# The first load of a batched product, made in eight transfers of 16 rows

## The chip, the core and the metric

The kernel runs on one core of a Trainium2 chip. Its metric is the device time of one execution in microseconds, the median of the runs shown. The core has five engines that run their own instruction queues: TensorE (PE), VectorE (DVE), ScalarE (ACT), GpSimd (POOL) and SyncE (SP). Data moves between the chip's main memory (HBM) and the on-chip memory of 128 partitions (SBUF) by 16 DMA engines; a transfer is issued from the queue of SyncE or ScalarE, and counts a semaphore up when it has landed.

## The reference

x and y have the shape 8 x 12 x 512 x 64, the result 8 x 12 x 512 x 512, all in float32:

```python
def reference(x, y):
    return np.einsum('bhtc,bhsc->bhts', x, y).astype(np.float32)
```

So there are 96 products of a 512 x 64 matrix with a 64 x 512 matrix. Inputs are 25.17 MB, the output is 100.66 MB.

## The kernel before, in words

The 96 products are taken in 6 groups of 16. Of each group there is one load of x and one of y, 12 loads in all, each 128 partitions x 4096 floats (2 MB, 16 KB for each partition, contiguous in HBM). Load n is of x for even n and of y for odd n. The results leave in 48 stores of the same size, 64 x 2 rows of 16 KB.

Loads and results share five buffers of 128 x 4096 floats (`slots`), handed out in turn by `slot()`. Each slot has a semaphore of its own for its transfers, `dma0` to `dma4`; a transfer adds 16 to it. The helper `emit` keeps books on who wrote and read what: before an instruction it puts the waits that it needs, and after it the semaphore increment. `ticks` holds the count that each semaphore will have reached, and a consumer waits for that count.

The order of the work is written out. `load(0)` to `load(4)` come first on SyncE's queue and need no wait, since the slots are empty. Then, for n from 0 to 11, `compress(n)` turns a load into bfloat16: ScalarE copies a load of x from its slot into `xk` (line 113), and a load of y is copied into `yb` in four pieces, two on VectorE, one on GpSimd, one on ScalarE. `mix` copies pieces of `xk` into `xb` so that pairs of values interleave; in the first part this is on GpSimd. When `compress(n)` has emptied a slot, `load(n + 5)` is issued into it: load 5 goes into slot 0 after ScalarE's copy of load 0.

`transposes` turns `xb` and `yb` on VectorE into the operands of the products, and `result` makes the products for one store: two times four matrix products of 128 x 512 (line 202) into PSUM, two copies from PSUM into a slot, mostly on ScalarE (line 113), and a store of the slot, from SyncE for two results in three and from ScalarE's queue for the third (and the last four).

The steps that the change touches are `load` (lines 127 to 134), of it the case n = 0, and through the semaphore count the wait of the instructions that read slot 0 (`copy`, line 110, and `need`, line 71).

Of the kernel before, what the change touches and what calls it, by code (L numbers as in the profile page):

```python
# [9 lines left out]
def kernel(  # L10
# [22 lines left out]
    nc = tc.nc  # L33
# [9 lines left out]
    K = 8  # L43
    E = R // K
    D = 32
    SLOTS = 5
    fp32 = mybir.dt.float32
    bf16 = mybir.dt.bfloat16
    u32 = mybir.dt.uint32
    COPY = mybir.ActivationFunctionType.Copy  # L50
    assert C == 2 * D and S == T and R == 2 * D and Q * V == D

    xv = x.rearrange("b h t c -> (b h t c)").rearrange("(g p n) -> g p n", p=P, n=R * C)
    yv = y.rearrange("b h t c -> (b h t c)").rearrange("(g p n) -> g p n", p=P, n=R * C)
# [5 lines left out]
    ps = ctx.enter_context(tc.tile_pool(name="ps", bufs=1, space=bass.MemoryType.PSUM))  # L60
    slots = [sb.tile([P, K * S], fp32, name=f"slot{i}") for i in range(SLOTS)]
    xks = [sb.tile([P, R, C], bf16, name=f"xk{i}") for i in range(NG - 1)]
    ybs = [[sb.tile([P, R // 2 * D], u32, name=f"yb{h}{i}") for i in range(NG - 1 + h)] for h in range(2)]
    xbs = [sb.tile([P, K * E * D], u32, name=f"xb{half}") for half in range(2)]
    xTs = [sb.tile([P, K * D * E], u32, name=f"xT{i}") for i in range(2)]
    yTs = [sb.tile([P, D * R // 2], u32, name=f"yT{i}") for i in range(2)]
    pms = [ps.tile([P, 4, S], fp32, name=f"pm{i}") for i in range(2)]
    engines = {"act": nc.scalar, "dve": nc.vector, "pool": nc.gpsimd, "pe": nc.tensor, "sp": nc.sync}
    sems, ticks, known, snaps, writer, readers = {}, {}, {e: {} for e in engines}, {}, {}, {}

    def need(name, points):

        best = {}
        for p, v in points:
            if known[name].get(p, 0) < v:
                best[p] = max(best.get(p, 0), v)
        for p, v in list(best.items()):
            if any(snaps[q, w].get(p, 0) >= v for q, w in best.items() if q != p):
                del best[p]
        for p, v in best.items():  # L80
            engines[name].wait_ge(sems[p], v)  # L81
            known[name][p] = v
            for q, w in snaps[p, v].items():
                known[name][q] = max(known[name].get(q, 0), w)

    def emit(name, make, reads=(), writes=(), dma=None):

        points = [writer[r] for r in (*reads, *writes) if r in writer]
        points += [v for w in writes for v in readers.get(w, ())]
        if name == "pool" and name in ticks:  # L90
            points.append((name, ticks[name]))
        need(name, points)
        p, step = (name, 1) if dma is None else (f"dma{dma}", 16)
        if p not in sems:
            sems[p] = tc.alloc_semaphore(p)
        make().then_inc(sems[p], step)
        at = (p, ticks.get(p, 0) + step)
        ticks[p] = at[1]
        snaps[at] = {**known[name], p: at[1]}
        if dma is None:  # L100
            snaps[at][name] = at[1]
        for r in reads:
            readers.setdefault(r, []).append(at)
        for w in writes:
            writer[w], readers[w] = at, []
# [14 lines left out]
    def both(i):  # L120
        return [("slot", i, 0), ("slot", i, 1)]

    def slot():
        made_slots.append(len(made_slots) % SLOTS)
        return made_slots[-1]

    def load(n):
        i = loaded[n] = slot()
        emit(
            "sp",  # L130
            lambda: nc.sync.dma_start(slots[i], (yv if n % 2 else xv)[n // 2]),  # L131
            writes=both(i),
            dma=i,
        )

    def compress(n):

# [8 lines left out]
        for half in range(2):  # L146
            b = g % (NG - 1 + half)
            yv2 = ybs[half][b].bitcast(bf16).rearrange("p (j c w) -> p j w c", j=R // 2, w=2)
            for ch in range(2):
                copy(  # L150
                    in_front[2 * half + ch],
                    yv2[ch * 64:(ch + 1) * 64],
                    ys[half * 64:(half + 1) * 64, :, ch * D:(ch + 1) * D].rearrange(
                        "p (j w) c -> p j w c", w=2
# [90 lines left out]
    with tc.tile_critical():  # L245
        for g in range(SLOTS):
            load(g)
        for half, name in enumerate(("dve", "pool")):
# [3 lines left out]
                writes=[("xb", half, part) for part in range(4)],  # L252
            )
        front = []
        for n in range(2 * NG):
            if n == 11:
                result(3, slot())
            compress(n)
            mix(n // 4, "pool", n % 4)
            if n == 4:  # L260
                transposes(0)
            if n < 5:
                load(n + SLOTS)
            elif n in (6, 8):
                load(n // 2 + 7)
            elif n < 10:
                front.append(slot())
            if n > 7 and n < 11:
                result(n - 8, front[n - 8])
            if n == 9:  # L270
                transposes(1)
# [38 lines left out]
```

## Time and profile before

| what | value |
|---|---|
| device time, median of 3 runs | 300.76 us (300.71 to 301.03) |
| span of the profiled execution, first to last instruction | 299.3 us |
| ScalarE / VectorE / TensorE / GpSimd busy | 204.2 / 160.8 / 131.2 / 56.0 us |
| DMA | 125.90 MB, mean 421 GB/s over the span |
| HBM read / written | 25.17 MB / 100.66 MB |
| first issue of a load | 0.95 us after the span's start |
| first copy of a landed load (ScalarE, xk) | 8.81 us |

The page gives busy times of each engine, then the span in 40 equal slices with the busy share in tenths, then the DMA queues. Of the profiled execution only the span is recorded; the time of a run is longer by what lies around the span, 300.76 - 299.3 = 1.46 us against the median. The timeline gives instructions in order of time, and the windows give the busy times and the moved bytes of chosen stretches. "SPq" marks an issue on SyncE's queue; "x <- y" is read "x written from y".

### The profile page before, as it was taken

The page shows a single profiled execution, that of the slowest core. Times are in us where ns is not written, and L with a number is a line of the kernel's source. Part 1 is how long each engine was busy: PE and PEld are TensorE (multiplying, and loading weights), DVE is VectorE, ACT ScalarE, POOL GpSimd, SP SyncE. Part 2 cuts the span into 40 slices and gives each one's busy share as a digit, 9 for nine tenths or more (in the row PEclk, how much of TensorE's full clock was granted, in tenths as well). Part 3 has the DMA queues.
Part 4 walks back from the last instruction along what each step waited for, and adds up shares of the span by engine and source line. Part 5 has one row for each costly group of instructions (what it writes and reads, how often), then busy time and mean ns, then how long its engine had stood idle before and what let it go on. Part 6 is the DMA issues. An engine that isn't in the chain of part 4 may idle for free.

```text
span 299.3 us, 1170 instructions
## 1 busy us (share of the span) xinstructions
PE 131.2 (44%) x384; PEld 35.2 (12%) x384; DVE 160.8 (54%) x77; ACT 204.2 (68%) x105; POOL 56.0 (19%) x23
## 2 busy tenths in 40 slices
PE   0000040557756665454655545464646473755100
PEld 0000010111111111111111111111111111111000
DVE  2167897999839590940946729219276330501400
ACT  1665676999999885677776868595959595459000
POOL 2399999991000000000000000000000000000000
PEclk9999999999599978596859597959597959587755
DMA  7999999999999999999999999999999999999995
GB/s 272 429 427 434 431 425 427 429 431 427 434 434 429 429 431 428 431 434 431 427 434 428 429 434 429 429 427 436 425 425 429 427 434 423 425 423 429 431 431 239
DMA packets 8645, 125.90 MB, mean 421 GB/s; under 512 B 960, under 2 KB 960, under 8 KB 960
## 3 DMA queue, kind: packets, MB, share of 16 engines
q1 hardware_dynamic: 6048, 88.08, 69.3%
q10 hardware_dynamic: 2592, 37.75, 29.6%
q8 instruction: 3, 0.05, 0.1%
q14 instruction: 2, 0.02, 0.0%
HBM read 25.17 MB, written 100.66 MB: 420 GB/s over the span
## 4 chain that ended last, share of the span: by engine, by line
DMA 57%; ACT 22%; PE 7%; issue 4%; DVE 3%; SPq 0%; ACTq 0%
DMA out_dram<-slot 44%; ACT slot L113 19%; DMA slot<-in_y_dram 7%; PE pm L202 7%; DMA slot<-in_x_dram 6%; DVE yb L115 2%; DVE slot L115 1%; ACT xk L113 1%; ACT yb L113 1%; SPq L131 0%; ACTq L81 0%; SPq L305 0%; SPq L245 0%
## 5 line engine op out<-in xcount | busy, mean ns | idle before, releaser
L113 ACT ACTIVATE slot<-pm 128x2048 f32<-128x2048 f32 x92 | 166.6, 1883 | 50.1 <-DMA out_dram<-slot 40.8
L202 PE MATMUL pm<-yT,xT 128*128 128x512 bf16 x384 | 131.2, 485 | 146.6 <-ACT slot L113 108.6
L180 DVE STREAM_TRANSPOSE xT<-xb 128x2048 uint32<-128x2048 uint32 x12 | 46.7, 3890 | 71.0 <-PE pm L202 68.6
L202 PEld LDWEIGHTS pm<-yT,xT 128*128 128x128 bf16 x384 | 35.2, 112 | 242.1 <-ACT slot L113 141.4
L115 DVE COPY xb<-xk 32x2048 bf16<-32x2048 bf16 x36 | 46.9, 1304 | 1.0
L115 DVE CAST yb<-slot 64x2048 bf16<-64x2048 f32 x12 | 36.1, 3012 | 17.0 <-DMA slot<-in_y_dram 16.8
L115 POOL COPY xb<-xk 32x2048 bf16<-32x2048 bf16 x12 | 36.2, 3019 | 10.5 <-ACT xk L113 9.7
L113 ACT ACTIVATE xk<-slot 128x4096 bf16<-128x4096 f32 x6 | 21.7, 3617 | 16.4 <-DMA slot<-in_x_dram 16.4
L115 DVE COPY slot<-pm 128x2048 f32<-128x2048 f32 x4 | 9.0, 2286 | 29.3 <-PE pm L202 29.3
L189 DVE STREAM_TRANSPOSE yT<-yb 128x1024 uint32<-128x1024 uint32 x12 | 23.2, 1932 | 0.0
L113 ACT ACTIVATE yb<-slot 64x2048 bf16<-64x2048 f32 x6 | 14.8, 2461 | 5.1 <-DMA slot<-in_y_dram 5.1
L115 POOL CAST yb<-slot 64x2048 bf16<-64x2048 f32 x6 | 17.8, 2968 | 1.3 <-DMA slot<-in_y_dram 0.8
L251 DVE MEMSET xb<- 128x2048 uint32 x1 | 1.8, 1765 | 1.4 <-SPq L245 1.4
L251 POOL MEMSET xb<- 128x2048 uint32 x1 | 1.8, 1804 | 0.5 <-SPq L245 0.5
L113 ACT ACT_TABLE_LOAD x1 | 1.3, 1283 | 0.9 <-SPq L245 0.9
L294 POOL MEMSET const-float32-0.0<- 128x1 f32 x1 | 0.1, 98 | 0.2 <-issue 0.2
L294 POOL MEMSET const-float32-1.0<- 128x1 f32 x1 | 0.1, 98 | 0.0
L294 POOL MEMSET const-bfloat16-1.0<- 128x1 bf16 x1 | 0.1, 98 | 0.0
L294 POOL MEMSET const-uint8-127<- 128x1 uint8 x1 | 0.1, 97 | 0.0
## 6 DMA issues: line engine op xcount, KB each, us to landing
out_dram<-slot SPq DMA_DIRECT2D x30, 2048.0 KB, 17.0
out_dram<-slot ACTq DMA_DIRECT2D x18, 2048.0 KB, 14.8
slot<-in_x_dram SPq DMA_DIRECT2D x6, 2048.0 KB, 17.6
slot<-in_y_dram SPq DMA_DIRECT2D x6, 2048.0 KB, 20.8
```

The source lines that it names most:

```text
L113: lambda: nc.scalar.activation(dst, src, COPY)
L115: else engines[name].tensor_copy(dst, src),
L180: lambda: nc.vector.transpose(xTs[half].rearrange("p (k r e) -> p k e r", k=K, e=E), xbs[half].rearrange("p (k e c) -> p k e c", k=K, e=E),),
L189: lambda: nc.vector.transpose(yTs[half].rearrange("p (r j) -> p j r", r=D), ybs[half][b].rearrange("p (j c) -> p j c", c=D),),
L202: last = nc.tensor.matmul(pms[k // 4][:, j, :], xT[:, k + j, h, :], yT[:, h * S:(h + 1) * S], start=True, stop=True,)
L251: lambda: engines[name].memset(xbs[half], 0.0),
L294: nc = _bacc.Bacc("TRN2", target_bir_lowering=False, num_devices=1)
```

## The change

Load 0, the first one of x, is issued as eight transfers instead of one. Transfer r (0 to 7) takes the partitions r, r + 8, r + 16, ..., r + 120: 16 rows of 16 KB. All eight add 16 to the semaphore of slot 0; the first seven do it directly, and `ticks` is set so that `emit` counts 128 for the last one. Every reader of slot 0 that waited for 16 waits for 128, and later counts of this semaphore are larger by 112. The other loads are as before.

```diff
+    W = 8
...
     def load(n):
         i = loaded[n] = slot()
-        emit(
-            "sp",
-            lambda: nc.sync.dma_start(slots[i], (yv if n % 2 else xv)[n // 2]),
-            writes=both(i),
-            dma=i,
-        )
+        src = (yv if n % 2 else xv)[n // 2]
+
+        def parts():
+
+            if n:
+                return nc.sync.dma_start(slots[i], src)
+            for r in range(W - 1):
+                nc.sync.dma_start(slots[i][r::W], src[r::W]).then_inc(sems["dma0"], 16)
+            ticks["dma0"] = 16 * (W - 1)
+            return nc.sync.dma_start(slots[i][W - 1::W], src[W - 1::W])
+
+        emit("sp", parts, writes=both(i), dma=i)
```

The order of the instructions on each engine's queue is otherwise the same: on SyncE the eight issues (lines 137 and 139 of the changed kernel) stand where the one stood (line 131), ahead of the four other first loads (line 135).

## The prediction

> **What bounds the kernel now.** I read the page's line of DMA shares and rates first, because the five engines are all far from full (ScalarE, the busiest, 68%).
>
> ```profile
> span 299.3 us, 1170 instructions
> ...
> PE 131.2 (44%) x384; PEld 35.2 (12%) x384; DVE 160.8 (54%) x77; ACT 204.2 (68%) x105; POOL 56.0 (19%) x23
> ...
> DMA  7999999999999999999999999999999999999995
> GB/s 272 429 427 434 431 425 427 429 431 427 434 434 429 429 431 428 431 434 431 427 434 428 429 434 429 429 427 436 425 425 429 427 434 423 425 423 429 431 431 239
> DMA packets 8645, 125.90 MB, mean 421 GB/s; under 512 B 960, under 2 KB 960, under 8 KB 960
> ```
>
> Of 40 slices only the first and the last are below nine tenths; the 38 between move 423 to 436 GB/s. The transfers never pause, so the time is: when the data begins to flow at full rate, plus 125.9 MB at that rate, plus the tail. Anything that costs transfer time in the first load is paid in full at the end, since no later slice has idle DMA time to take it up; and a compute engine that starts later costs nothing until it lets the queue of transfers run dry.
>
> Next the opening, by the windows of the first microseconds. After window and length come PE, PEld, DVE, ACT and POOL, the clock, the DMA share (above 1 because a packet is booked where it starts) and GB/s.
>
> ```profile
> 1.00:2.00 1.00, 0.00 (x0) 0.00 (x0) 0.56 (x1) 1.00 (x1) 1.00 (x1) 1.00 0.09 33
> 2.00:3.00 1.00, 0.00 (x0) 0.00 (x0) 1.00 (x1) 0.18 (x1) 0.75 (x1) 1.00 1.57 279
> 3.00:4.00 1.00, 0.00 (x0) 0.00 (x0) 0.21 (x1) 0.00 (x0) 0.00 (x0) 1.00 0.49 197
> 4.00:5.00 1.00, 0.00 (x0) 0.00 (x0) 0.00 (x0) 0.00 (x0) 0.00 (x0) 1.00 1.00 426
> ...
> 7.00:8.00 1.00, 0.00 (x0) 0.00 (x0) 0.00 (x0) 0.00 (x0) 0.00 (x0) 1.00 1.04 442
> 8.00:9.00 1.00, 0.00 (x0) 0.00 (x0) 0.00 (x0) 0.19 (x1) 0.00 (x0) 1.00 0.92 393
> 9.00:10.00 1.00, 0.00 (x0) 0.00 (x0) 0.00 (x0) 1.00 (x1) 0.00 (x0) 1.00 1.11 475
> ```
>
> Data flows from about 2.0 us, but until 4.0 us at (279 + 197) / 2 = 238 GB/s, a little over half. This is the only stretch in which the DMA engines have work and do not deliver.
>
> Last, the timelines of SyncE's queue and of ScalarE (start, duration, what).
>
> ```profile
> 0.95 0.39 SPq L131 DMA_DIRECT2D slot<-in_x_dram  x1
> 1.40 0.42 SPq L131 DMA_DIRECT2D slot<-in_y_dram  x1
> 1.86 0.43 SPq L131 DMA_DIRECT2D slot<-in_x_dram  x1
> 2.33 0.66 SPq L131 DMA_DIRECT2D slot<-in_y_dram  x1
> 3.04 0.49 SPq L131 DMA_DIRECT2D slot<-in_x_dram  x1
> 12.46 0.33 SPq L131 DMA_DIRECT2D slot<-in_y_dram  x1
> ```
>
> ```profile
> 8.81 3.62 ACT L113 ACTIVATE xk<-slot 128x4096 bf16<-128x4096 f32 x1 [6.63 <-DMA slot<-in_x_dram]
> 13.69 2.44 ACT L113 ACTIVATE yb<-slot 64x2048 bf16<-64x2048 f32 x1 [1.26 <-DMA slot<-in_y_dram]
> 18.58 3.62 ACT L113 ACTIVATE xk<-slot 128x4096 bf16<-128x4096 f32 x1 [2.45 <-DMA slot<-in_x_dram]
> ```
>
> The five first loads are issued by 3.53 us and land one after another: ScalarE starts on them at 8.81, 13.69, 18.58, so one load of 2,097 KB takes 4.89 us, 429 GB/s. Load 5 is issued at 12.46, when ScalarE has emptied slot 0.
>
> **The change, part by part.** The sum is made against this execution: its span is 299.3, the median of the three timed runs is 300.76, so 1.46 us lie around the span; I keep them and add every difference to 300.76.
>
> *The rate of the first load.* Before, load 0 has 33 + 279 + 197 = 509 KB moved by 4.00 us, and the other 1,588 KB take 1,588 / 429 = 3.70 us: done at 7.70. Afterwards the same 128 rows of 16 KB move, but as sets of 16 whose partitions are 8 apart. Every transfer in this trace covers all 128 partitions, so no row shows whether 16 rows at that spacing are taken in at 429 GB/s. The bounds are the fastest and the slowest rates that the trace has under load. Fast end: 429 from the first byte, 2,064 / 429 = 4.81 us after 2.0, done at 6.81, a gain of 0.89. Neutral: as before, 0. Slow end: the 197 GB/s of the window from 3 to 4 us held throughout, 2,064 / 197 = 10.48, done at 12.48, a loss of 4.78. At the 238 of the whole opening it is 8.67, done at 10.67, a loss of 2.97. I take the middle of the last two, **+3.9 us**. The reason is the nearest row: the opening is the one place where the DMA engines all work on their first few rows at once, which is what the change makes of the whole first load, and there they give half rate; the full rate is only seen in stretches where they are spread over the rows of 128-partition transfers. That is an argument by likeness and not a measurement, hence the chance below. Both ends stay for the range.
>
> [...]
>
> *Seven more issues on SyncE.* Issues of 128 rows start 0.45, 0.46, 0.47 and 0.71 us apart; the price of one of 16 rows is not in the trace, bounded by nothing and 0.71. The DMA engines need 16 x 16,384 B / 429 GB/s = 0.61 us for a set, so at 0.46 the queue stays ahead of them: 0. At 0.71 it would fall behind by 8 x 0.10 = 0.8 us. I take 0, since three of the four distances are below 0.61. Queued behind on SyncE are loads 1 to 4. They move back by 7 x 0.46 = 3.2 us, load 1 to 4.6; its data is wanted at 7.70, and first data followed issue by 2.0 - 0.95 = 1.05 us, so 2 us of cover are left (none at 0.71: 6.6 + 1.05 = 7.7). Load 5 waits for ScalarE and not for these issues.
>
> *Seven more completions.* 960 packets under 512 B in 60 transfers are 16 each; 7 x 16 = 112 come on top. The boundary between load 0 and load 1 lies in the windows from 7 to 10 us, whose mean is 437: nothing lost, so 0. Upper end: if the dip to 393 (0.08 us) were a boundary's price, 7 x 0.08 = 0.56.
>
> *The wait of ScalarE.* Its copy of slot 0 into xk now waits for 128 counts on the slot's semaphore instead of 16, so for the last of the eight transfers. With load 0 at 11.6 instead of 7.7, the copy starts at 12.7 and ends at 16.3, and load 5, behind it, is issued at 16.4. Loads 1 to 4 then keep the DMA engines busy until 11.6 + 4 x 4.89 = 31.2, so nothing runs dry. Behind the copy on ScalarE are the yb copy of load 1, whose data is late by as much, and on GpSimd the first xb copies, which wait for xk. All of this moves by the same 3.9 us as the transfers; relative to them nobody is later, and the full DMA slices mean that nobody was waited for that could now hide it.
>
> Sum: 300.76 + 3.9 + 0 + 0 = 304.66, told as **304.7**.
>
> **The rivals.**
>
> *The rate is kept* (no change): if each DMA engine's own pace is the limit, 0.61 us for a row of 16 KB, then the same rows take the same 128 turns. For it: loads alone and mixes of loads and stores both give 423 to 436 GB/s, as a limit of the engines would. Against it: the opening, where engines with work run at half. Time 300.8, with the small costs up to 301.2.
>
> *The first data comes earlier* (faster). Place: the 1.05 us from the first issue to the first data, and the half-rate opening. If preparing a transfer costs by its rows, 16 rows instead of 128 save 7/8 of the 0.39 us issue, 0.34; if the opening was slow because so many rows were asked for at once, up to 0.89 more. Both: 300.76 - 1.23 = 299.5; I would expect some two thirds, 299.9. It decides when more than half of the 1.23 comes true, with the rate kept. Against it: issues of the same size take 0.33 to 0.66 us, so the issue's time seems to depend on other things than rows. [...]
>
> *SyncE can't feed them* (a little slower): the issues come every 0.71 us, or the completions cost; +0.8 and +0.56 as above, 301.4 to 302.1. For it: the one issue that took 0.66. A rate between half and full falls here too, up to 303.6.
>
> *The change doesn't do what it says*: a set of 16 rows could go to a few DMA engines instead of all 16. On 8 engines it gives the half rate of the forecast; on one, 128 x 0.61 = 78 us for the load, about 370. All transfers of 128 rows use 16, so I give the extreme 1 in 100.
>
> **How the numbers follow.** Half rate, 304.7: 0.47. Its own range is 303.6 to 305.7 (from +2.97 to +4.78 with a little around it). Rate kept, within 0.2%: 0.20. Earlier data, faster by over 0.2%: 0.23. SyncE, completions or a partial loss, 301.4 to 303.6: 0.09; the extreme 0.01. So faster 0.23, same 0.20, slower 0.57; 0.2% is 0.6 us, about what runs of this kernel (300.71 to 301.03) can tell from no change. The range goes from 300.0 to 305.8: it holds the half rate, the partial losses and the kept rate (0.76) and, of the earlier data, the part down to 300.0 (0.05); the rest of the gains and the extreme, 0.19, are left out.
>
> **What would show it.** Half rate: the windows from 2 to 11 us stand near 200 to 240 GB/s, then 429; ScalarE's first copy starts near 12.7; all later slices are as before, and the span is 303.2. Kept rate: the first copy starts at 8.8 within a few tenths, and 426 from 4 us on. Earlier data: more than 33 GB/s between 1 and 2 us, or 400 and more between 2 and 4, and the copy starts at 8.2 or sooner. SyncE: issues 0.61 us or more apart and DMA shares below 1 between them. In each case 960 + 112 = 1,072 packets are under 512 B; fewer would mean that sets do not use all 16 engines. The prediction is wrong if 16 rows spaced by 8 are taken in as fast as 128 rows, since then nothing slow is left in it.

## The result, and the profile after

The changed kernel takes 305.68 us (305.49 to 305.75, 4 runs), the kernel before on the same chip 300.89 (300.71 to 301.35, 4 runs). The ratio is 1.0156, with a 95% interval of 1.0144 to 1.0168: slower by 4.79 us. The forecast was 304.7, with a range from 300.0 to 305.8.

The page of the changed kernel: span, the slices of the DMA engines, the packets, and the issue row of the new transfers.

```profile
span 303.8 us, 1177 instructions
...
DMA  7999999999999999999999999999999999999995
GB/s 173 276 425 436 416 434 429 431 431 423 440 423 438 425 434 426 436 427 434 429 434 425 437 423 436 425 438 425 436 423 438 423 431 427 419 438 425 421 438 231
DMA packets 8757, 125.90 MB, mean 414 GB/s; under 512 B 1072, under 2 KB 1072, under 8 KB 1072
...
slot<-in_x_dram SPq DMA_DIRECT2D x8, 256.0 KB, 5.8
```

The shares of busy DMA time (tenths of each of the 40 slices) are digit for digit those of before. What changed is what the busy engines bring: 173 and 276 GB/s in the first two slices (7.6 us each) instead of 272 and 429. From the third slice on nothing is different. So the DMA line alone hides this loss: from 3 to 12 us the share was 1.03 in the changed kernel, at 219 GB/s, and 0.94 before, at 402. The line below it shows the loss. The 1,072 small packets are 960 + 112, which fits eight transfers that each complete on 16 DMA engines.

Windows of the changed kernel (length, the five engines, the clock, DMA share, GB/s):

```profile
1.00:2.00 1.00, 0.00 (x0) 0.00 (x0) 0.56 (x1) 1.00 (x1) 1.00 (x1) 1.00 0.00 0
2.00:3.00 1.00, 0.00 (x0) 0.00 (x0) 1.00 (x1) 0.18 (x1) 0.75 (x1) 1.00 0.92 262
3.00:4.00 1.00, 0.00 (x0) 0.00 (x0) 0.21 (x1) 0.00 (x0) 0.00 (x0) 1.00 1.12 262
...
13.00:14.00 1.00, 0.00 (x0) 0.00 (x0) 0.00 (x0) 0.72 (x1) 0.00 (x0) 1.00 1.00 426
```

The same nine microseconds in both kernels, first before, then after:

```profile
3.00:12.00 9.00, 0.00 (x0) 0.00 (x0) 0.21 (x1) 3.19 (x1) 0.00 (x0) 1.00 0.94 402
```

```profile
3.00:12.00 9.00, 0.00 (x0) 0.00 (x0) 0.21 (x1) 0.00 (x0) 0.00 (x0) 1.00 1.03 219
```

219 GB/s is half of the 429 of full flow (0.51). The packets in the trace say it row by row: between 4 and 11 us a row of 16 KB takes 0.611 us in the kernel before (median) and 1.26 us in the changed one, with 16 rows under way at any time in both. At 13 us, when load 0 is through, 426 GB/s are back.

The timelines of SyncE's queue and of ScalarE in the changed kernel:

```profile
0.96 4.42 SPq L137 DMA_DIRECT2D slot<-in_x_dram  x7
5.42 0.59 SPq L139 DMA_DIRECT2D slot<-in_x_dram  x1
6.05 0.58 SPq L135 DMA_DIRECT2D slot<-in_y_dram  x1
```

```profile
13.28 3.62 ACT L114 ACTIVATE xk<-slot 128x4096 bf16<-128x4096 f32 x1 [11.09 <-DMA slot<-in_x_dram]
18.09 2.45 ACT L114 ACTIVATE yb<-slot 64x2048 bf16<-64x2048 f32 x1 [1.20 <-DMA slot<-in_y_dram]
22.98 3.62 ACT L114 ACTIVATE xk<-slot 128x4096 bf16<-128x4096 f32 x1 [2.45 <-DMA slot<-in_x_dram]
```

ScalarE's first copy starts 13.28 - 8.81 = 4.47 us later, the next two 4.40 later, and the span is 303.8 - 299.3 = 4.5 longer. The delay that load 0 leaves behind stays much the same to the end.

The packets show where it arises. The first row starts at 2.36 us instead of 1.98 (0.38 later). The last row of load 0 is through at 12.39 instead of 8.44 (3.95 later). Full rate does not return at once behind it: the first 16 rows of load 1, which is whole, still take 0.86 to 1.20 us instead of 0.61. When 4.2 MB have arrived, the stream of rows is 4.56 us behind that of the kernel before, and from there on mostly 4.2 to 4.7 to the end.

### The profile page after: what moved, and what is told of

It reads as the page before. It is cut to its first block, busy times and chain, and to the rows that moved or that the text cites. A ratio compares the mean times of both kernels' runs of the same rounds, so it can differ in the third digit from the quotient of the medians.

```text
span 303.8 us, 1177 instructions
## 1 busy us (share of the span) xinstructions
PE 129.8 (43%) x384; PEld 35.2 (12%) x384; DVE 160.9 (53%) x77; ACT 204.1 (67%) x105; POOL 56.1 (18%) x23
## 2 busy tenths in 40 slices
DMA packets 8757, 125.90 MB, mean 414 GB/s; under 512 B 1072, under 2 KB 1072, under 8 KB 1072
## 4 chain that ended last, share of the span: by engine, by line
DMA 56%; ACT 22%; PE 6%; issue 4%; DVE 3%; SPq 2%; ACTq 0%
DMA out_dram<-slot 43%; ACT slot L114 20%; DMA slot<-in_y_dram 7%; DMA slot<-in_x_dram 6%; PE pm L209 6%; DVE yb L116 2%; DVE slot L116 1%; SPq L137 1%; ACT xk L114 1%; ACT yb L114 1%; SPq L135 0%; SPq L139 0%; ACTq L82 0%; SPq L312 0%; SPq L252 0%
## 5 line engine op out<-in xcount | busy, mean ns | idle before, releaser
L209 PE MATMUL pm<-yT,xT 128*128 128x512 bf16 x384 | 129.8, 482 | 152.3 <-ACT slot L114 108.8
```

Source lines behind the costliest of these rows:

```text
L209: last = nc.tensor.matmul(pms[k // 4][:, j, :], xT[:, k + j, h, :], yT[:, h * S:(h + 1) * S], start=True, stop=True,)
```

## The experiments

Four theories were to be told apart. P: the partitions that rows go to fall into groups, and rows under way to the same group share that group's rate. S: splitting costs as such, one row at a time with a completion behind it. H: reading rows 128 KB apart in HBM is slow. Q: SyncE cannot issue fast enough. Each ratio below is against runs of the kernel before that were made beside it: a median of 300.91 us for the columns, the other rows, the neighbours and the halves, 300.93 for the combs, the sixteen transfers and the opening, 301.12 for the last two. In the diffs `...` stands for lines left out; the last transfer, which stands on a line of its own, changes as the others do.

**The same eight, over all partitions.** Against the changed kernel:

```diff
-                nc.sync.dma_start(slots[i][r::W], src[r::W])
+                nc.sync.dma_start(slots[i][:, r * 512:(r + 1) * 512], src[:, r * 512:(r + 1) * 512])
...
```

> Load 0 in eight transfers again, but each of all 128 partitions and an eighth of the columns (512 floats, 2 KB of each row). The number of transfers, their bytes and their completions are those of the changed kernel; the spacing of the partitions is gone. Theory P (the rate belongs to groups of destination partitions, and sets spaced by 8 reach half of them): full rate again, 300.3 to 301.5, ScalarE's first copy at 8.5 to 9.5 us. Rival S (the splitting itself costs: one piece at a time for each DMA engine, with a completion behind each): 305.7 as with the change. Rival Q (SyncE cannot issue eight transfers fast enough): issues 0.63 us apart and about 301 to 302. By P a loss of up to 1 us from pieces of 2 KB would still fit.

Measured: 302.47 us against 300.91, ratio 1.0055 (1.0034 to 1.0075), first copy at 10.55. Most of the loss is gone, but not all, and the time lies above the range of P. The window from 3 to 9 us:

```profile
3.00:9.00 6.00, 0.00 (x0) 0.00 (x0) 0.21 (x1) 0.00 (x0) 0.00 (x0) 1.00 0.99 289
```

289 GB/s is 0.67 of full rate, so this form has a price of its own. The run alone does not say whether that is the pieces of 2 KB or the number of transfers, and it refutes S only in its full size. Q does not explain the rest: the eight issues start 0.45 to 0.49 us apart, less than the 0.61 that such a set needs at full rate.

**Other rows of HBM, same destinations.** Transfer r reads rows 16r to 16r + 15:

```diff
-                nc.sync.dma_start(slots[i][r::W], src[r::W])
+                nc.sync.dma_start(slots[i][r::W], src[r * (P // W):(r + 1) * (P // W)])
...
```

> The eight transfers keep their destinations (partitions r, r + 8, ...), but read 16 consecutive rows of 16 KB each instead of rows 128 KB apart, so the rows of the first group of x land on other partitions than their own and its products are those of permuted rows; the work is the same. Theory P: nothing changes, 305.2 to 306.0, first copy near 13.3 us. Rival H (the loss comes from reading rows 128 KB apart in HBM at once): back to 300.3 to 301.5, first copy near 8.8.

Measured: 305.40 us, ratio 1.0147 (1.0132 to 1.0162), first copy at 13.05.

```profile
3.00:12.00 9.00, 0.00 (x0) 0.00 (x0) 0.21 (x1) 0.00 (x0) 0.00 (x0) 1.00 1.02 226
```

The half rate stays with neighbouring sources. H falls: where the rows come from makes no difference that shows here.

**Neighbours on both sides.** Eight transfers of 16 rows to partitions 16r to 16r + 15:

```diff
-                nc.sync.dma_start(slots[i][r::W], src[r::W])
+                nc.sync.dma_start(slots[i][r * (P // W):(r + 1) * (P // W)], src[r * (P // W):(r + 1) * (P // W)])
...
```

> Eight transfers of 16 consecutive rows to 16 consecutive partitions. [...] Theory P with groups of 8 neighbours: 2 of 16 groups, some 38 us for the load, 333. Rival S: as the change, 305.7, since number, size and completions are the same. Rival H: not slower than 305.7.

Measured: 313.02 us, ratio 1.0400 (1.0385 to 1.0416), first copy at 20.64. A window, then SyncE's queue:

```profile
3.00:18.00 15.00, 0.00 (x0) 0.00 (x0) 0.21 (x1) 0.00 (x0) 0.00 (x0) 1.00 1.06 122
```

```profile
0.96 3.16 SPq L137 DMA_DIRECT2D slot<-in_x_dram  x7
4.16 0.42 SPq L140 DMA_DIRECT2D slot<-in_x_dram  x1
```

Number, size and completions of the transfers are those of the changed kernel, and yet the loss is 12.1 us instead of 4.79. S and Q cannot make that: SyncE issued faster here (the eight in 3.62 us instead of 5.05). Groups of 8 neighbours (333 us) are out as well. What arrives is 122 GB/s, 0.28 of the 429 of full flow, so other destinations gave another rate. A row takes 2.246 us (median of the 48 packets between 4 and 11 us), 3.7 times the 0.611 of the kernel before.

**Two halves.** Only two transfers, partitions 0 to 63 and 64 to 127:

```diff
-    W = 8
+    W = 2
...
-                nc.sync.dma_start(slots[i][r::W], src[r::W])
+                nc.sync.dma_start(slots[i][r * (P // W):(r + 1) * (P // W)], src[r * (P // W):(r + 1) * (P // W)])
...
```

> Load 0 in two transfers only, partitions 0 to 63 and 64 to 127. [...] Rivals S and Q: two transfers cost a quarter or less of what eight cost, at most 302.

Measured: 305.69 us, ratio 1.0157 (1.0142 to 1.0172), first copy at 13.37.

```profile
3.00:12.00 9.00, 0.00 (x0) 0.00 (x0) 0.21 (x1) 0.00 (x0) 0.00 (x0) 1.00 1.01 211
```

The whole loss with two transfers instead of eight, and two issues that were over by 2.2 us; S and Q allowed 302. They fall as the cause of this loss.

**Every second partition.** The counterpart: two transfers of 64 rows again, the even and the odd partitions. Against the changed kernel only W changes:

```diff
-    W = 8
+    W = 2
```

> Load 0 in two transfers of 64 rows, the even and the odd partitions. [...]

Measured: 301.47 us, ratio 1.0016 (1.0007 to 1.0025), first copy at 8.89. The window from 4 to 8 us:

```profile
4.00:8.00 4.00, 0.00 (x0) 0.00 (x0) 0.00 (x0) 0.00 (x0) 0.00 (x0) 1.00 1.01 426
```

Two halves and two combs have the same number of transfers, rows, bytes and completions; they differ in which partitions stand together, and with that in the rows of HBM, which made no difference above. The halves run at 211 GB/s (3 to 12 us), the comb at 426 (4 to 8), and 4.2 us lie between them. This pair, with the other rows of HBM, settles that the destinations decide. That much of P is shown; which partitions slow each other down, and by what, no run shows. The comb is not quite free either: it costs 0.5 us, which is clear of its interval.

**Every fourth partition.** Four transfers of 32 rows:

```diff
-    W = 8
+    W = 4
```

> Load 0 in four transfers of 32 rows, partitions r, r + 4, r + 8 and so on. [...] Rival S (number of transfers) expects about 303.

Measured: 301.78 us, ratio 1.0028 (1.0019 to 1.0038), below the 303 of S.

```profile
4.00:8.00 4.00, 0.00 (x0) 0.00 (x0) 0.00 (x0) 0.00 (x0) 0.00 (x0) 1.00 0.98 328
```

328 GB/s is 0.76 of full rate, where the comb of two has 426 in the same window. Between 4 and 11 us the median row takes 0.611 us, but the slowest 5% 1.2 us or more. Which rows are slow, and why, is open.

**Sixteen transfers of 8 rows.** Each takes eight partitions 4 apart within 32 neighbours, the first one 0, 4, ..., 28:

```diff
-    W = 8
+    W = 16
...
-                nc.sync.dma_start(slots[i][r::W], src[r::W])
+                nc.sync.dma_start(slots[i][32 * (r // 4) + r % 4:32 * (r // 4) + 32:4], src[32 * (r // 4) + r % 4:32 * (r // 4) + 32:4])
...
```

> [...] Rival S (a row with a completion behind it is slow by itself): rows take 1.26 us as with the change, on half the engines, so the load needs some 20 us and the time is about 315.

Measured: 309.68 us, ratio 1.0289 (1.0273 to 1.0304), first copy at 16.85. Windows, then SyncE's queue:

```profile
3.00:13.00 10.00, 0.00 (x0) 0.00 (x0) 0.20 (x1) 0.00 (x0) 0.00 (x0) 1.00 0.48 182
```

```profile
0.96 10.22 SPq L137 DMA_DIRECT2D slot<-in_x_dram  x15
11.22 0.62 SPq L140 DMA_DIRECT2D slot<-in_x_dram  x1
11.89 0.44 SPq L135 DMA_DIRECT2D slot<-in_y_dram  x1
```

The median row takes 0.611 us, as in the kernel before, and not the 1.26 of S; a share of 0.48 gives 182 GB/s, where the changed kernel needs 1.03 for 219. The time is 4.0 us above the changed kernel's all the same: here Q is real. Fifteen issues take 10.22 us, 0.68 each, more than the 0.61 of a row, so SyncE sets the pace, and load 1 is not issued before 11.89. That is not all of the loss: from 13 to 16 us, when rows of load 1 run beside the last sets, 229 to 262 GB/s arrive at a share near 1 (0.96 to 1.02). Why is open; no run tests it.

**The opening.** The kernel before, with loads 1 to 4 behind VectorE's memset:

```diff
-        for g in range(SLOTS):
-            load(g)
+        load(0)
         for half, name in enumerate(("dve", "pool")):
...
+        need("sp", [("dve", 1)])
+        for g in range(1, SLOTS):
+            load(g)
```

> The kernel before, with loads 1 to 4 issued only after VectorE's memset has ended (near 3.2 us) and not right behind load 0. It asks what slows the opening, which the prediction used as the likeness for half rate. If the issues of the next loads disturb the first rows, the windows from 2 to 4 us rise from 238 towards 429 GB/s and the time falls to 299.9 to 300.3. If the first rows are slow by themselves, the windows stay near 238 and the time stays at 300.6 to 301.1.

Measured: 300.95 us, ratio 1.0001 (0.9991 to 1.0010).

```profile
2.00:3.00 1.00, 0.00 (x0) 0.00 (x0) 1.00 (x1) 0.19 (x1) 0.75 (x1) 1.00 1.33 246
3.00:4.00 1.00, 0.00 (x0) 0.00 (x0) 0.21 (x1) 0.00 (x0) 0.00 (x0) 1.00 0.68 246
```

246 GB/s with load 0 alone on the queue until 3.24 us, 238 before: it is not the issues of the next loads that slow the first rows. The partitions of the transfer do not explain it either, since the same transfer covers all 128 and has 410 GB/s from 4 to 6 us (the mean of 393 and 426). What does is open. It differs with the form of the transfer: the first 16 rows take 1.47 us (median) in the kernel before, 1.54 here, and 0.88 in the changed kernel.

**Two halves of the columns.**

```diff
-    W = 8
+    W = 2
...
-                nc.sync.dma_start(slots[i][r::W], src[r::W])
+                nc.sync.dma_start(slots[i][:, r * 2048:(r + 1) * 2048], src[:, r * 2048:(r + 1) * 2048])
...
```

> Load 0 in two transfers of all 128 partitions and half of the columns each, so in pieces of 8 KB. The eight column transfers measured 302.47, 1.56 above the kernel before, with 289 GB/s from 3 to 9 us. If that came from the size of the pieces (2 KB), pieces of 8 KB give 300.7 to 301.3 and more than 400 GB/s from 4 to 8 us. If every additional transfer costs (seven cost 1.56, so 0.22 each), about 301.15 by one more transfer; the rate between 4 and 8 us then tells: it would stay full.

Measured: 301.04 us against 301.12, ratio 1.0000 (0.9991 to 1.0010).

```profile
4.00:8.00 4.00, 0.00 (x0) 0.00 (x0) 0.00 (x0) 0.00 (x0) 0.00 (x0) 1.00 1.03 436
```

Splitting by columns at 8 KB costs nothing that shows, and 436 GB/s is full rate. That leaves the 1.56 us of the eight column transfers to their pieces of 2 KB or to their number; one more transfer would be 0.2 us, too little for this interval to exclude. The first copy starts at 8.48 instead of 8.81, and the time does not move; with an interval of 0.3 us to either side, the run cannot tell a gain of that size.

**The same eight for load 2.**

```diff
-            if n:
+            if n != 2:
```

Here the counts are on the semaphore of slot 2 (`dma2`).

> The same eight transfers of 16 rows, but for load 2 and not for load 0, which is whole again. Load 2 comes while the DMA engines are long in full flow, and its issues lie under the two loads before it. Theory P: the loss belongs to where the rows go, and any full stretch pays it: 305.0 to 305.9, with half rate for some 9.5 us between 12 and 23 us and ScalarE's first copy back at 8.8. Rival O (the loss belongs to the opening of the program, late first data and slow first rows): 300.7 to 301.5.

Measured: 306.29 us against 301.12, ratio 1.0173 (1.0158 to 1.0188), slightly above the range of P. ScalarE's timeline and the slices:

```profile
8.71 3.62 ACT L114 ACTIVATE xk<-slot 128x4096 bf16<-128x4096 f32 x1 [6.53 <-DMA slot<-in_x_dram]
14.25 2.45 ACT L114 ACTIVATE yb<-slot 64x2048 bf16<-64x2048 f32 x1 [1.92 <-DMA slot<-in_y_dram]
23.90 3.62 ACT L114 ACTIVATE xk<-slot 128x4096 bf16<-128x4096 f32 x1 [7.20 <-DMA slot<-in_x_dram]
```

```profile
14.00:21.00 7.00, 0.00 (x0) 0.00 (x0) 5.13 (x2) 2.45 (x1) 6.80 (x3) 1.00 1.00 215
```

Load 0 is on time (8.71), and the half rate has moved with the change into the middle of full flow: 215 GB/s from 14 to 21 us, ScalarE's copy of load 2 at 23.90 instead of 18.58. The opening is not the cause; the place that the rows go to is.

No version beat the kernel before by more than its interval: the late issues and the two column halves are level with it.

## Why the prediction was right

*What bounds the kernel* held. The slices from the third on are full in both kernels, and 4.47 us at the first copy are 4.5 us of span at the end. The same sets in full flow, for load 2, cost 5.17 us, so the loads around it gave no cover either.

*The rate of the first load* carried the result, and its +3.9 us was 0.9 too small. For load 0 itself the term was right: its last row came 3.95 us later (at 12.39 instead of 8.44; the prediction's 7.70 and 11.6 count packets where they start). The parts were others, though. The first row came 0.38 later, which the prediction had at nothing (0 GB/s between 1 and 2 us in place of 33), and the rows took 3.57 longer. The mis-sized part lies behind load 0: the prediction let full rate return with its last row, but the first 16 rows of load 1 still took 0.86 to 1.20 us, and the stream of rows was 4.56 us late behind them. Likewise ScalarE's copy started 0.89 us after the last row and not 0.37, so at 13.28 and not at 12.7. Why the slowness lasts beyond the slow load is open.

Between the 4.5 us of the spans and the 4.79 of the timed runs lie 0.3 us that single executions differ by (300.71 to 301.35). The forecast span of 303.2 was too short for the same reason: its 1.46 us around the span set the median time against the span of one execution. Where both are known of the same execution, 1.73 to 1.92 us lie around it in the kernel before and in all others but the sixteen transfers (305.63 - 303.8 = 1.83 for the changed one).

*The reason given for it* was only a likeness, and the likeness was wrong: late issues did not remove the slow opening (246 GB/s against 238), and its transfers cover all partitions. That the middle of the opening's two rates, 217.5 GB/s, fell on the half rate (219 from 3 to 12 us) was luck. What the runs show in its place is that the destinations decide: 219 GB/s at steps of 8, 211 for 64 neighbours, 122 for 16 neighbours, 426 for every second partition and 328 for every fourth. What in the destinations does it, no run shows. The measured 4.79 stands at the prediction's slow end, 4.78 at 197 GB/s throughout, but by another sum: load 0 itself was only 3.95 late, its first rows were faster than those before (0.88 against 1.47 us), and the rest came from the later first data and from the rows behind load 0.

*Seven more issues* were costed at nothing, by the 0.46 us between issues of 128 rows. They came 0.63 us apart. That is a little over the 0.61 that a set needs at full rate, but at half rate a set needs 1.2, so it was hidden under the slower rows. With the sixteen small transfers a pace of 0.68 was the bound. The cover of load 1 was there: issued at 6.05 and not at 4.6, but wanted only after 12.

*Seven more completions* cost nothing that can be seen: two halves, with 16 more counts on the semaphore instead of 112, lose as much as eight sets do (305.69 and 305.68 us).

*The wait of ScalarE* moved as described, by 4.47 us where 3.9 was forecast, and the copies behind it by 4.40. Nothing ran dry.

*The rivals.* The kept rate and the earlier first data did not happen; the first data came later. This split let nothing start sooner: its first row starts 0.38 us later, and the copy waits for all eight anyway. With the two column halves the first copy is 0.33 us earlier, without a gain in time. Of the signs of SyncE as the bound the first one showed (issues 0.61 us or more apart), but not the shares below 1; the bound it was only in the run with sixteen transfers. By the 1,072 small packets the sets did use all 16 DMA engines.

## What to carry to other kernels

Choose the partitions of a split transfer by where its rows go and not by how many DMA engines they occupy: sets of sixteen rows ran at half rate here with destinations 8 apart (219 GB/s), and at little more than a quarter with 16 neighbours (122). If a transfer has to be split, every second partition (0.5 us lost) or halves of the columns (no loss that shows) kept the rate; halves of the partitions lost 4.8 us. In a kernel whose DMA line is full everywhere, read the GB/s below it: the load at 219 GB/s had a share of 1.03 here. Expect a lost microsecond at the end, as here, where 4.47 us at the first copy were 4.5 us of span.

## What was not expected

Issues have two prices, and the number of rows does not order them. Issues of 128 rows at a time, and of 16 neighbouring rows, mostly follow each other in 0.43 to 0.49 us, and the first data comes 1.0 us after the first one starts. With 8, 16, 32 or 64 rows at a step, and also with 64 neighbours, it is mostly 0.6 to 0.7 us, and the first data comes 1.4 us after the start (1.6 with 8 rows). The cause was not looked for further.

In the run with neighbours a row takes 2.246 us, 3.7 times the 0.611 of the kernel before, and in the changed kernel 1.26, 2.1 times. If a whole number of rows shared a fixed rate, as P would have it, these would be whole multiples; 3.7 is not one. Why is open.

The slowness outlasts the slow load. With neighbours the first 16 rows of load 1 take 1.38 to 1.76 us, and the stream of rows falls behind by another 1.2 us while load 1 arrives; with every second partition they take 0.61, and it does not. The cause was not looked for.
